# Grouped attention's weighted sums with the weights stationary and the values moving, on one Trainium2 core

## The chip, the core and the metric

The program runs on one core of a Trainium2 chip. The core has five engines that run their own instruction streams: TensorE (PE, matrix multiplications; the loading of its stationary operand is listed apart as PEld), VectorE (DVE), ScalarE (ACT), GpSimd (POOL) and SyncE (SP, which here only issues transfers). TensorE writes into PSUM, eight banks of 128 x 512 floats here; VectorE and ScalarE read PSUM and write SBUF. The metric is the device time of one execution in microseconds; several executions are timed and their median is taken. One execution is also recorded by the hardware profiler, and every row below comes from that record.

## The reference, cut to what matters

The model is a trunk of four layers with 256 positions and 2048 features. Layer 0 and layer 3 use latent attention; layer 1 uses grouped attention over keys that an indexer selects ("sparse"); layer 2 uses grouped attention in a sliding window with a learned sink per head. Each layer also has four heads of cross-attention to a memory, and the joined head outputs are multiplied by SiLU(gate) and projected back.

The change is in layers 1 and 2 alone. Both have 32 query heads of 64 features in 4 groups; the 8 heads of a group share one key head and one value head. For one head, in the window layer:

```python
s = q @ k.T * 64**-0.5 + bias          # 256 x 256, masked
m = max(rowmax(s), sink)
e = exp(s - m)
p = e / (rowsum(e) + exp(sink - m))    # a factor per row (query)
o = p @ v                              # weighted sum of the values, 256 x 64
...
y = concat(o of all heads, memory heads) * silu(gate)
x = x + y @ w_out
```

The factor of a row is the same for all keys of that row, so it can stand before or after the product with v. The sparse layer has no sink and takes its mask from the selection.

## The kernel before

Everything is computed in two parts of reduced width: a float32 matrix is split into a high part `hi` (what the type fp32r keeps) and a low part `lo` (the rest), by `split` (L58 to L64): ScalarE copies into `hi` (L60), VectorE subtracts (L64). A product is then hi*hi + hi*lo + lo*hi, three matrix multiplications in fp32r. The weights of every projection are split in that way on the fly: SyncE loads them (`stage`), `parts_of` makes `wh` and `wl` (three buffers each), and `rows_by` (L227 to L229) or `columns_by` (L246, L250) multiplies. These projections are most of TensorE's work.

For grouped attention the class `Grouped` has `first` (keys, values, and in the sparse layer the selection), `project(g)` (queries, the table of biases and the gate of group g) and `attend(g)`. A layer does memory part 4, groups 0 to 3, memory part 5, and after each part the output projection `w_out` of the part before it. No order of instructions is written out by hand here: the framework's planner sets the order on each engine before the program runs, from its own costs, earlier lines of the program first where their operands are ready. So the heads of a group are spread among the matrix multiplications of the previous part's `w_out` and of the next group's `project`.

`attend` handles one head at a time, the queries in two halves b of 128 (the second half has two key tiles, the first only one, because of causality):

- scores (L786, L789) in PSUM tiles `sp`;
- `masked_softmax` (L434): bias, row minimum of the negated scores (L445, L447), exponential with row sums (L452), reciprocal of the sums `rc` (L468 with a sink, L470 without), then `normalized`: ScalarE multiplies each half of `e` by its rows' factors (two ACTIVATE e<-e,rc through L60);
- `weights_T` (L427): three transposes of 128x128 blocks by TensorE into the PSUM tile `ptp`, float32;
- split of `ptp` into `pT` (high, ScalarE) and `hl` (low, VectorE), 128 x 384 each, keys on the partitions;
- the weighted sums (L811): six matrix multiplications into PSUM `o`. The values are stationary: `vz` is a buffer per part, with zero columns between the value heads so that a slice of 128 columns gives the head's 64 features either in the lower or in the upper half of the 128 output partitions (head pairs stack). The transposed weights move: 256 columns for key tile 0, 128 for key tile 1, each three times (hi*hi, hi*lo, lo*hi). The result has features on the partitions and queries along the columns, which is the layout of the gate;
- after four heads, `gated` (L415): `o` times the gate, and split into `y`.

PSUM has four buffers `mp` for `sp`, `ptp`, `o` and the transposes of the queries, and four `acc` for the projections. `o` is held over four heads. The tags of the work buffers that matter: `e` (4 buffers of 128 x 256: u, e, bs, th), `z` (3, used by the gate), `t512` (3).

`first` zeroes both `vz` with GpSimd (L689, 128 x 1152 elements each) and splits the values into them.

Of the kernel before, what the change touches and what calls it, by code (L numbers as in the profile page):

```python
# [8 lines left out]
F32 = mybir.dt.float32  # L9
F32R = mybir.dt.float32r  # L10
# [5 lines left out]
P = 128  # L16
S = 256
# [14 lines left out]
def kernel(ctx: ExitStack, tc: tile.TileContext, a: dict, out: bass.AP,  # L32
                             kinds=(0, 1, 2, 0)):
    nc = tc.nc
# [3 lines left out]
    act = ctx.enter_context(tc.tile_pool(name="act", bufs=1))  # L38
    wk = ctx.enter_context(tc.tile_pool(name="wk", bufs=1))
# [3 lines left out]
    def misc(name, dt=F32):  # L43
        return ps.tile([P, 512], dt, name=name, tag="mp", bufs=4)

    def tmp(name, n=512, dt=F32):
        return wk.tile([P, n], dt, name=name, tag=f"t{n}", bufs=3)

    def small(name, n, dt=F32, bufs=None):
        return wk.tile([P, n], dt, name=name, tag=f"s{n}" if bufs is None else name,  # L50
                       bufs=bufs or 6)

    def f32(ap):
        return ap.bitcast(F32)

    def part_tile(dt=F32R):
        return wk.tile([P, 512], dt, name="hl", tag="hl", bufs=3)

    def copy_act(o, i, scale=1.0):
        nc.scalar.activation(o, i, AF.Copy, scale=scale)  # L60

    def split(hi, lo, src):
        copy_act(hi, src)
        nc.vector.tensor_sub(lo, src, f32(hi))  # L64
# [19 lines left out]
    ident = cst.tile([P, P], F32, name="ident")  # L84
# [328 lines left out]
    def gated(y, o, gT, j):  # L413
        yt = tmp("yt")
        nc.vector.tensor_mul(yt, o, gT[:, j:j + 2, :].rearrange("p a b -> p (a b)"))  # L415
        y3 = yt.rearrange("p (a b) -> p a b", a=2)
        split(y[:, 0, j:j + 2, :], y[:, 1, j:j + 2, :], y3)


    def normalized(e, r, n):  # L420
        copy_act(e[:, :n], e[:, :n], scale=r)

    def weights_T(es, blocks):

        tp = misc("ptp")
        for i, (b, k) in enumerate(blocks):
            nc.tensor.transpose(tp[:, i * P:(i + 1) * P], es[b][:, k * P:(k + 1) * P], ident)  # L427
        return tp

    def attend(o, v, pT):  # L430
        nc.tensor.matmul(o, v[0], pT[:, :S], start=True, stop=False)
        nc.tensor.matmul(o[:, P:], v[1], pT[:, S:S + P], start=False, stop=True)

    def masked_softmax(score, bias, scale=None, nsk=None):  # L434


        es = []
        mn, sm = small("mn", 2), small("sm", 2)
        for b in range(2):
            n = (b + 1) * P  # L440
            sp = score(b)
            u = wk.tile([P, S], F32, name="u", tag="e", bufs=4)
            bi = bias(b, n)
            if b == 0:
                nc.vector.tensor_add(u[:, :n], sp[:, n:2 * n], bi)  # L445
                bi = u[:, :n]
            nc.vector.tensor_tensor_reduce(u[:, :n], sp[:, :n], bi, -1.0,  # L447
                                           nsk if nsk is not None else BIG,
                                           op0=OP.add, op1=OP.min, accum_out=mn[:, b:b + 1])
            e = wk.tile([P, S], F32, name="e", tag="e", bufs=4)  # L450
            if scale is None:
                nc.scalar.activation(e[:, :n], u[:, :n], AF.Exp, bias=mn[:, b:b + 1], scale=-1.0,  # L452
                                     accum_out=sm[:, b:b + 1])
            else:
                ms = small("ms", 2)
                nc.vector.tensor_mul(ms[:, :1], mn[:, b:b + 1], scale[0][:, b:b + 1])
                nc.scalar.activation(e[:, :n], u[:, :n], AF.Exp, bias=ms[:, :1],
                                     scale=scale[1][:, b:b + 1], accum_out=sm[:, b:b + 1])
            es.append(e)
        r = small("rc", 2)  # L460
        if nsk is not None:
            d = small("sd", 2)
            nc.vector.tensor_scalar(d, mn, nsk, None, op0=OP.subtract)
            e2 = small("se", 2)
            nc.scalar.activation(e2, d, AF.Exp)
            s3 = small("sa", 2)
            nc.vector.tensor_add(s3, sm, e2)
            nc.vector.reciprocal(r, s3)  # L468
        else:
            nc.vector.reciprocal(r, sm)  # L470
        for b in range(2):
            normalized(es[b], r[:, b:b + 1], (b + 1) * P)
        return weights_T(es, [(0, 0), (1, 0), (1, 1)])


# [188 lines left out]
    class Grouped:  # L664
# [7 lines left out]
        def first(self):  # L672
            nm, w = self.nm, self.w
            acc = rows_by(nm.at, 16, w, 0, (self.kv0, 512), "kv")
            self.k = act.tile([P, 4, 2, S], F32R, name="kd", tag="big0")
            vs = act.tile([P, 4, S], F32, name="vs", tag="aux", bufs=AUX)
            self.v, self.sel = vs[:, :2, :], vs[:, 2:, :]
            for t in range(2):
                sc = nm.col("rstd", t)
                self.dup(lambda i0, i1: self.k.rearrange("p g v s -> p (g v) s")  # L680
                         [:, i0:i1, t * P:(t + 1) * P], acc[t][:, :S], sc, 4)
                copy_act(self.v[:, t, :], acc[t][:, S:], scale=sc)
            if self.sparse:
                self.select()


            self.vz = [act.tile([P, 2, 9 * 64], F32R, name="vz", tag=f"big{1 + z}") for z in range(2)]
            for z in range(2):
                nc.gpsimd.memset(f32(self.vz[z]), 0.0)  # L689
            for t in range(2):  # L690
                hi, lo = (self.vz[z][:, t, 64:].rearrange("p (g c) -> p g c", c=P)[:, :, :64] for z in range(2))
                split(hi, lo, self.v[:, t, :].rearrange("p (g c) -> p g c", c=64))

        def dup(self, dst, src, sc, n):

# [83 lines left out]
        def attend(self, g, q, bm, gT):  # L779
            y = act.tile([P, 2, 4, S], F32R, name="y", tag="y", bufs=2)  # L780
            for h in range(8):
                def score(b):
                    sp = misc("sp")
                    qb = q[h // 4][:, h % 4, b * P:(b + 1) * P]
                    if b == 0:
                        nc.tensor.matmul(sp[:, :S], qb, self.k[:, g, :, :P], start=True, stop=True)  # L786
                    else:
                        for v in range(2):
                            nc.tensor.matmul(sp[:, :S], qb, self.k[:, g, v, :],  # L789
                                             start=v == 0, stop=v == 1)  # L790
                    return sp

                def bias(b, n):
                    bh = bm[:, h, S - n:]
                    if not self.sparse:
                        return bh
                    bs = wk.tile([P, S], F32, name="bs", tag="e", bufs=4)
                    nc.vector.tensor_add(bs[:, :n], bh, self.sel[:, b, :n])
                    return bs[:, :n]
                nsk = None if self.sparse else nsink[:, g * 8 + h:g * 8 + h + 1]  # L800
                tp = masked_softmax(score, bias, None, nsk)
                pH, pL = wk.tile([P, 512], F32R, name="pT", tag="pT", bufs=2), part_tile()
                split(pH[:, :3 * P], pL[:, :3 * P], tp[:, :3 * P])
                if h % 4 == 0:
                    o = misc("o")
                c0 = (h // 2 % 2) * S
                v0 = g * P + (64 if h % 2 == 0 else 0)
                for t in range(2):
                    ks = slice(t * S, t * S + S - t * P)
                    for n_, (z, p_) in enumerate(((0, pH), (0, pL), (1, pH))):  # L810
                        nc.tensor.matmul(o[:, c0 + t * P:c0 + S], self.vz[z][:, t, v0:v0 + P], p_[:, ks],  # L811
                                         start=h % 2 == t == n_ == 0, stop=h % 2 == t == 1 and n_ == 2)
                if h % 4 == 3:
                    gated(y, o, gT, (h // 4) * 2)
            return y


# [3 lines left out]
    for i in range(depth):  # L821
# [23 lines left out]
        for n_, part in enumerate(order):  # L845
            if part >= 4:
                y = memory_attend(*memory_project(nm, i, mixer.w, mixer.mq0, mixer.g0, part - 4))
            else:
                y = mixer.attend(*mixer.project(part))
# [89 lines left out]
```

## Time and profile before

| | |
|---|---|
| Median of 3 runs | 2635.05 us (2634.15 to 2639.67) |
| Profiled execution, its own time | 2636.8 us |
| Its span, first to last instruction | 2634.7 us |
| TensorE busy | 2601.2 us (99%) |
| VectorE busy | 1884.1 us (72%) |
| ScalarE busy | 1628.8 us (62%) |
| GpSimd busy | 57.3 us (2%) |
| Mean granted TensorE clock | 0.997 |
| Heads of grouped attention, sparse layer | about 1144 to 1484 us from the span's start |
| The same, window layer | about 1640 to 1976 us |

How to read it: a matrix multiplication's duration in a row is from its start to its modelled end, and several are in flight at once, so durations don't add up; what one costs TensorE is the step from its start to the start of the next. A row of the timeline with "x2" holds two consecutive instructions of the same line. "128x256" behind a multiplication is its output, so 256 moving columns. A load (LDWEIGHTS) runs beside the multiplication before it.

### The profile page before, as it was taken

How to read it: one execution, taken by the hardware profiler on the slowest of the kernel's cores; microseconds unless marked ns; L12 is line 12 of the kernel's file. 1: busy time of each engine (PE TensorE's matmuls, PEld its weight loads, DVE VectorE, ACT ScalarE, POOL GpSimd, SP SyncE). 2: the span in 40 equal slices, each digit the busy share in tenths (PEclk: the TensorE clock that was granted, in tenths of full speed). 3: DMA queues.
4: the chain of work that ended last, by engine and by line, in shares of the span. 5: the costliest groups of instructions: out<-in, count | busy, mean ns of one | idle time of the engine just before them, and what ended most of it. 6: DMA issues, size and time to landing. Idle time of an engine off the chain costs nothing.

```text
span 2634.7 us, 42943 instructions
## 1 busy us (share of the span) xinstructions
PE 2601.2 (99%) x14556; PEld 2254.7 (86%) x14556; DVE 1884.1 (72%) x4171; ACT 1628.8 (62%) x3476; POOL 57.3 (2%) x101
## 2 busy tenths in 40 slices
PE   8999999999999999999999999999999999999998
PEld 7888888888888889888888888888888888888886
DVE  6566656677767685877777776777778767776767
ACT  6455556556656566666666666676666655665655
POOL 1000000000000000000000000000000000000000
PEclk9999999999999999999999999999999999999999
DMA  9889886666557665555555555555555666655764
GB/s 305 279 287 300 281 256 198 166 185 168 169 160 224 192 192 172 167 183 170 173 163 191 188 190 177 173 172 178 189 168 162 205 165 186 165 170 156 226 183 135
DMA packets 456924, 511.70 MB, mean 194 GB/s; under 512 B 69584, under 2 KB 352480, under 8 KB 455552
## 3 DMA queue, kind: packets, MB, share of 16 engines
q1 hardware_dynamic: 443328, 451.75, 56.5%
q0 software_dynamic: 13088, 56.16, 6.6%
q8 instruction: 114, 1.87, 0.3%
q14 instruction: 106, 0.87, 0.1%
q10 hardware_dynamic: 288, 1.05, 0.1%
HBM read 489.91 MB, written 31.56 MB: 198 GB/s over the span
## 4 chain that ended last, share of the span: by engine, by line
PE 97%; DMA 1%; DVE 1%; ACT 0%; issue 0%; SPq 0%; ACTq 0%
PE acc_g L246 14%; PE acc_g L250 7%; PE acc_wo L227 7%; PE acc_wo L228 7%; PE acc_wo L229 7%; PE acc_mq L246 5%; PE acc_mk L246 5%; PE acc_qn L246 3%; PE acc_cq L246 3%; PE acc_mq L250 2%; PE acc_mk L250 2%; PE acc_q L227 2%; PE acc_q L228 2%; PE acc_q L229 2%; PE acc_mv L227 2%; PE acc_mv L228 2%
## 5 line engine op out<-in xcount | busy, mean ns | idle before, releaser
L64 DVE TENSOR_TENSOR wl<-wr,wh 128x512 fp32r<-128x512 f32 (+2 forms) x1776 | 1173.8, 664 | 645.1 <-ACT wh L60 614.2
L60 ACT ACTIVATE wh<-wr 128x512 fp32r<-128x512 f32 (+2 forms) x1776 | 1079.0, 609 | 837.3 <-PE acc_g L246 183.7
L246 PE MATMUL acc_g<-xT,wh 128*128 128x512 f32 x1536 | 489.0, 397 | 0.6 <-DVE z L257 0.6
L250 PEld LDWEIGHTS acc_g<-xT,wl 128*128 128x128 f32 x1536 | 285.2, 188 | 60.7
L250 PE MATMUL acc_g<-xT,wl 128*128 128x256 f32 x1536 | 311.0, 280 | 0.0
L228 PE MATMUL acc_wo<-wl,y 128*128 128x512 f32 x768 | 302.6, 394 | 0.6 <-DVE wl L64 0.5
L229 PE MATMUL acc_wo<-wh,y 128*128 128x512 f32 x768 | 299.1, 390 | 0.0
L246 PEld LDWEIGHTS acc_g<-xT,wh 128*128 128x128 f32 x1536 | 238.1, 189 | 4.8 <-issue 1.1
L227 PE MATMUL acc_wo<-wh,y 128*128 128x512 f32 x768 | 240.4, 393 | 0.7 <-ACT wh L60 0.6
L228 PEld LDWEIGHTS acc_wo<-wl,y 128*128 128x128 f32 x768 | 144.3, 188 | 30.0 <-DVE wl L64 1.4
L229 PEld LDWEIGHTS acc_wo<-wh,y 128*128 128x128 f32 x768 | 144.2, 188 | 28.4
L227 PEld LDWEIGHTS acc_wo<-wh,y 128*128 128x128 f32 x768 | 141.3, 188 | 27.8 <-ACT wh L60 1.0
L246 PE MATMUL acc_mk<-mT,wh 128*128 128x512 f32 x512 | 161.9, 398 | 2.4 <-ACT wh L60 2.4
L246 PE MATMUL acc_mq<-xT,wh 128*128 128x512 f32 x512 | 161.7, 397 | 0.0
L832 DVE TENSOR_TENSOR x<-x,acc_wo 128x512 f32<-128x512 f32 x192 | 125.7, 683 | 7.1 <-PE acc_wo L229 6.8
L246 PE MATMUL acc_qn<-cT,wh 128*128 128x512 f32 x384 | 123.2, 399 | 0.0
L246 PE MATMUL acc_cq<-xT,wh 128*128 128x512 f32 x384 | 120.8, 396 | 0.0
L250 PEld LDWEIGHTS acc_mk<-mT,wl 128*128 128x128 f32 x512 | 96.7, 189 | 23.4 <-DVE wl L64 0.8
L250 PEld LDWEIGHTS acc_mq<-xT,wl 128*128 128x128 f32 x512 | 93.7, 188 | 20.0
L250 PE MATMUL acc_mq<-xT,wl 128*128 128x256 f32 x512 | 102.5, 281 | 0.0
L228 PE MATMUL acc_q<-wl,xT 128*128 128x512 f32 x256 | 102.4, 400 | 0.0
L250 PE MATMUL acc_mk<-mT,wl 128*128 128x256 f32 x512 | 101.7, 280 | 0.0
(280 smaller groups left out, 4438.0 us busy)
## 6 DMA issues: line engine op xcount, KB each, us to landing
wr<-in_w_out_dram SPq DMA_DIRECT2D x192, 512.0 KB, 3.7
wr<-in_w_in_a_dram SPq DMA_DIRECT2D x176, 512.0 KB, 4.1
wr<-in_w_mem_kv_dram SPq DMA_DIRECT2D x128, 512.0 KB, 5.6
wr<-in_w_in_b_dram SPq DMA_DIRECT2D x112, 512.0 KB, 3.5
wr<-in_w_in_c_dram SPq DMA_DIRECT2D x104, 512.0 KB, 3.5
wr<-in_w_uq_dram SPq DMA_DIRECT2D x288, 128.0 KB, 2.6
tab<-flat POOLq DMA_DIRECT2D x8, 1536.0 KB, 11.1
wr<-in_w_in_a_dram SPq DMA_DIRECT2D x32, 288.0 KB, 3.0
```

The costliest lines, as they stand in the source:

```text
L60: nc.scalar.activation(o, i, AF.Copy, scale=scale)
L64: nc.vector.tensor_sub(lo, src, f32(hi))
L227: nc.tensor.matmul(acc[t][:, :n], xh, wh[:, :n], start=first, stop=False)
L228: nc.tensor.matmul(acc[t][:, :n], xh, wl[:, :n], start=False, stop=False)
L229: nc.tensor.matmul(acc[t][:, :n], xl, wh[:, :n], start=False, stop=last)
L246: nc.tensor.matmul(acc[j], wh[:, o:o + P], q[:, :, kt % 4, :], start=kt == 0, stop=False)
L250: nc.tensor.matmul(acc[j][:, 0, :], wl[:, o:o + P], q[:, 0, kt % 4, :], start=False, stop=kt == kts - 1)
L832: nc.vector.tensor_add(xs, xs, acc[t])
```

## The change

The weighted sums are turned round. The transposed weights `pH`, `pL` become the stationary operand, one 128 x 128 block per load, and the values' parts move: `vv` holds for each group 64 columns of the high part and 64 of the low part side by side, so one multiplication with `pH` stationary and 128 moving columns gives hi*hi and hi*lo in two halves, and one with `pL` stationary and 64 moving columns adds lo*hi to the second half. Three blocks per head give again six multiplications. The result now has queries on the partitions. So the rows' factor can be applied to the sums instead of to `e`: `normalized` is no longer called for these heads. After two heads ScalarE copies the second halves out of PSUM (`lo`), VectorE adds the first halves (`su`) and multiplies by the factors into `yr`; after four heads four transposes by TensorE (float32, into a PSUM tile `ot`) bring the layout with features on the partitions back, and `gated` reads `ot` instead of `o`. `o` is allocated every two heads. `vz` and its zeroing by GpSimd go.

```diff
-    def masked_softmax(score, bias, scale=None, nsk=None):
+    def masked_softmax(score, bias, scale=None, nsk=None, r=None):
...
-        r = small("rc", 2)
+        later = r is not None
+        if not later:
+            r = small("rc", 2)
...
-        for b in range(2):
-            normalized(es[b], r[:, b:b + 1], (b + 1) * P)
+        if not later:
+            for b in range(2):
+                normalized(es[b], r[:, b:b + 1], (b + 1) * P)
...
-            self.vz = [act.tile([P, 2, 9 * 64], F32R, name="vz", tag=f"big{1 + z}") for z in range(2)]
-            for z in range(2):
-                nc.gpsimd.memset(f32(self.vz[z]), 0.0)
-            for t in range(2):
-                hi, lo = (self.vz[z][:, t, 64:].rearrange("p (g c) -> p g c", c=P)[:, :, :64] for z in range(2))
-                split(hi, lo, self.v[:, t, :].rearrange("p (g c) -> p g c", c=64))
+            self.vv = act.tile([P, 2, 4, 2, 64], F32R, name="vv", tag="big1")
+            for t in range(2):
+                split(self.vv[:, t, :, 0, :], self.vv[:, t, :, 1, :],
+                      self.v[:, t, :].rearrange("p (g c) -> p g c", c=64))
...
             for h in range(8):
+                if h % 2 == 0:
+                    o = misc("o")[:].rearrange("p (b h v d) -> p b h v d", b=2, h=2, v=2)
+                    r = small("rc4", 4, bufs=3)[:].rearrange("p (b h) -> p b h", b=2)
+                if h % 4 == 0:
+                    yr = tmp("yr")[:].rearrange("p (b h d) -> p b h d", b=2, h=4)
...
-                tp = masked_softmax(score, bias, None, nsk)
+                tp = masked_softmax(score, bias, None, nsk, r[:, :, h % 2])
                 pH, pL = wk.tile([P, 512], F32R, name="pT", tag="pT", bufs=2), part_tile()
                 split(pH[:, :3 * P], pL[:, :3 * P], tp[:, :3 * P])
-                if h % 4 == 0:
-                    o = misc("o")
-                c0 = (h // 2 % 2) * S
-                v0 = g * P + (64 if h % 2 == 0 else 0)
-                for t in range(2):
-                    ks = slice(t * S, t * S + S - t * P)
-                    for n_, (z, p_) in enumerate(((0, pH), (0, pL), (1, pH))):
-                        nc.tensor.matmul(o[:, c0 + t * P:c0 + S], self.vz[z][:, t, v0:v0 + P], p_[:, ks],
-                                         start=h % 2 == t == n_ == 0, stop=h % 2 == t == 1 and n_ == 2)
+                for n_, (b, t) in enumerate(((0, 0), (1, 0), (1, 1))):
+                    ks = slice(n_ * P, (n_ + 1) * P)
+                    nc.tensor.matmul(o[:, b, h % 2].rearrange("p v d -> p (v d)"), pH[:, ks],
+                                     self.vv[:, t, g].rearrange("p v d -> p (v d)"),
+                                     start=t == 0, stop=False)
+                    nc.tensor.matmul(o[:, b, h % 2, 1, :], pL[:, ks], self.vv[:, t, g, 0, :],
+                                     start=False, stop=t == b)
+                if h % 2 == 1:
+                    lo = wk.tile([P, S], F32, name="ol", tag="z", bufs=3)[:].rearrange(
+                        "p (b h d) -> p b h d", b=2, h=2)
+                    su = wk.tile([P, S], F32, name="os", tag="z", bufs=3)[:].rearrange(
+                        "p (b h d) -> p b h d", b=2, h=2)
+                    copy_act(lo, o[:, :, :, 1, :])
+                    nc.vector.tensor_add(su, lo, o[:, :, :, 0, :])
+                    nc.vector.tensor_mul(yr[:, :, h % 4 - 1:h % 4 + 1, :], su,
+                                         r[:, :, :, None].to_broadcast([P, 2, 2, 64]))
                 if h % 4 == 3:
-                    gated(y, o, gT, (h // 4) * 2)
+                    ot = misc("ot")
+                    for j in range(2):
+                        for b in range(2):
+                            nc.tensor.transpose(ot[:, j * S + b * P:j * S + (b + 1) * P],
+                                                yr[:, b, 2 * j:2 * j + 2, :].rearrange("p h d -> p (h d)"),
+                                                ident)
+                    gated(y, ot, gT, (h // 4) * 2)
```

## Prediction

> **What bounds the kernel now.** I read the page's totals and its chain of waits first, then the busy times of the two stretches in which grouped attention runs, then who waited for whom there, and last the timeline of single instructions, because only steps from start to start price a matrix multiplication.
>
> ```profile
> span 2634.7 us, 42943 instructions
> ...
> PE 2601.2 (99%) x14556; PEld 2254.7 (86%) x14556; DVE 1884.1 (72%) x4171; ACT 1628.8 (62%) x3476; POOL 57.3 (2%) x101
> ...
> PE 97%; DMA 1%; DVE 1%; ACT 0%; issue 0%; SPq 0%; ACTq 0%
> ```
>
> ```profile
> core 0: us, PE busy (x) PEld busy (x) DVE busy (x) ACT busy (x) POOL busy (x), PEclk, DMA share, GB/s
> 1144.00:1554.00 410.00, 407.03 (x2210) 347.45 (x2209) 315.32 (x732) 268.26 (x592) 8.37 (x11) 1.00 0.56 177
> 1637.00:2036.00 399.00, 396.97 (x2207) 341.34 (x2206) 304.89 (x730) 266.54 (x623) 5.93 (x9) 1.00 0.55 173
> ```
>
> TensorE is busy 99% of the span and makes up 97% of the chain that ended last. In the two stretches with the heads it is idle for 410.00 - 407.03 + 399.00 - 396.97 = 5.0 us of 809, at full clock. VectorE is busy (315.32 + 304.89) / 809 = 77%, ScalarE 66%. So work that leaves or joins VectorE and ScalarE is worth nothing by itself; what counts is the time that TensorE needs for its instructions, and the few waits it has. Those of the stretch from 1144 to 2036 us, by engine and line, total, times and longest:
>
> ```profile
> PE o L811 <- ACT pT L60: 1.7, 3, 0.6
> PE ptp L427 <- ACT e L60: 1.4, 3, 0.5
> PE acc_g L246 <- DVE z L257: 0.6, 3, 0.2
> PE acc_wo L227 <- ACT wh L60: 0.6, 1, 0.6
> PE acc_wo L228 <- DVE wl L64: 0.5, 1, 0.5
> ```
>
> They are small: the planner has put projection work between the links of a head's chain nearly everywhere.
>
> **The weighted sums.** Moving columns per head go from 3 x 256 + 3 x 128 = 1152 to 3 x 128 + 3 x 64 = 576, loads stay at six. The timeline of one head's six multiplications and of their loads:
>
> ```profile
> 1195.86 0.39 PE L229 MATMUL acc_q<-wh,xT 128*128 128x512 f32 x1
> 1196.09 0.28 PE L811 MATMUL o<-pT,vz 128*128 128x256 f32 x1
> 1196.20 0.28 PE L811 MATMUL o<-hl,vz 128*128 128x256 f32 x1
> 1196.32 0.34 PE L811 MATMUL o<-pT,vz 128*128 128x256 f32 x2
> 1196.50 0.28 PE L811 MATMUL o<-hl,vz 128*128 128x128 f32 x1
> 1196.61 0.28 PE L811 MATMUL o<-pT,vz 128*128 128x128 f32 x1
> 1196.72 0.68 PE L227 MATMUL acc_q<-wh,xT 128*128 128x512 f32 x2
> 1197.24 0.40 PE L228 MATMUL acc_q<-wl,xT 128*128 128x512 f32 x1
> ```
>
> ```profile
> 1196.44 0.19 PEld L811 LDWEIGHTS o<-hl,vz 128*128 128x128 f32 x1
> 1196.55 0.19 PEld L811 LDWEIGHTS o<-pT,vz 128*128 128x128 f32 x1
> 1196.66 0.30 PEld L227 LDWEIGHTS acc_q<-wh,xT 128*128 128x128 f32 x2
> ```
>
> A multiplication with 512 columns takes 1196.09 - 1195.86 = 0.23 us from start to start. From the head's first multiplication to the acc_q of L228 at 1197.24, 1.15 us pass, of which the two acc_q of L227 would take 0.46 in a row: the six cost 0.69 us. With 256 columns the step is 0.115 us; with 128 columns it isn't half of that but 0.11 (1196.50 to 1196.61), because the loads follow each other no closer than 0.11 us. Halving the columns therefore buys almost nothing: six loads at 0.11 are 0.66 us. No row shows 64 moving columns in this type; the nearest on either side are the 128 columns above and a sum over features that moves a single column, four in a row:
>
> ```profile
> 478.55 0.53 PEld L592 LDWEIGHTS cqp<-ones,cqs 128*128 128x128 f32 x4
> 479.00 0.30 PEld L246 LDWEIGHTS acc_mq<-xT,wh 128*128 128x128 f32 x2
> ```
>
> (479.00 - 478.55) / 4 = 0.113 us per load with one column, so 0.11 to 0.113 holds from both ends, and six cost 0.66 to 0.68 us. I take 0.665, a gain of 0.025 us per head, 64 heads: 1.6 us (0.6 to 1.9).
>
> **The transposes of the sums.** Two layers x 32 heads / 4 x 4 = 64 float32 transposes of 128x128 more, the same operation as `ptp`. Four in a row by the timeline:
>
> ```profile
> 1991.84 0.60 PE L427 MATMUL ptp<-ident,e 128*128 128x128 f32 x4
> 1992.19 0.70 PE L227 MATMUL acc_wo<-wh,y 128*128 128x512 f32 x2
> 1992.73 0.39 PE L228 MATMUL acc_wo<-wl,y 128*128 128x512 f32 x1
> ```
>
> 1992.73 - 1991.84 - 2 x 0.23 = 0.43 us for four, x 16 = 6.9 us. They fill TensorE's own queue and nothing covers them. The row gives each a duration of 0.27 us behind the start of the last, but it overlaps what follows. [...]
>
> TensorE's sum: 6.9 - 1.6 = +5.3 us.
>
> **ScalarE, VectorE, GpSimd.** Rows of the groups kept apart by shape (busy us, mean ns of one):
>
> ```profile
> L60 ACT ACTIVATE e<-e,rc 128x256 f32<-128x256 f32 x128 | 61.9, 495 | 0.0
> L406 DVE TENSOR_TENSOR hz<-z,half 128x256 f32<-128x256 f32 x96 | 40.5, 422 | 1.5
> L257 DVE TENSOR_TENSOR z<-z,acc_g 128x256 f32<-128x256 f32 x96 | 39.8, 415 | 1.6 <-ACT z L60 1.6
> L60 ACT ACTIVATE e<-e,rc 128x128 f32<-128x128 f32 x96 | 37.4, 390 | 1.2 <-DVE rc L468 0.9
> L60 ACT ACTIVATE z<-acc_g 128x256 f32<-128x256 f32 x96 | 35.2, 367 | 0.0
> L689 POOL MEMSET vz<- 128x1152 f32 x4 | 4.2, 1063 | 158.1 <-PE isp L745 130.9 <-ACT rl L748 16.9 <-PE o L811 10.3
> ```
>
> Gone per pair of heads: four e<-e,rc, 2 x (0.495 + 0.390) = 1.77 us of ScalarE. New: `lo`, like z<-acc_g, 0.37 on ScalarE; `su`, like z<-z,acc_g, 0.42, and the product with the factors, like hz<-z,half, 0.42 on VectorE (the strided and the broadcast operand have no row of exactly this form; between 0.42 and twice that). Over 32 pairs ScalarE loses 45 us and VectorE gains 27 (to 54), which makes it (620 + 27) / 809 = 80%, 83% at the upper bound. TensorE covers both. The cover is thinnest where heads and `w_out` fall together:
>
> ```profile
> 1164.00:1184.00 20.00, 20.00 (x97) 16.70 (x97) 17.02 (x41) 12.58 (x28) 0.00 (x0) 1.00 0.58 184
> ```
>
> There VectorE already has 17.0 of 20 us; one pair more of products is 17.9, still under 20, with three buffers of `wl` ahead of TensorE. I book nothing. The four memsets (1.06 us) and their waits are GpSimd's alone, whose queue otherwise only issues transfers; nobody in the list of TensorE's waits waits for it. The split of the values has as many elements as before. Nothing on SP's queue moves.
>
> **Waits.** The transposes of `e` no longer wait for ScalarE's product with `rc`: the row of 1.4 us goes, and the head's chain is 0.9 us shorter. Against it, TensorE's queue now holds 16 times four transposes that wait for `lo`, `su`, the product: three links of 0.37 + 0.42 + 0.42 = 1.2 us and what stands ahead of them in two queues (0.6 to 0.7 us per split of the weights), and behind them in TensorE's queue stand the projection and the next head's scores. If the planner puts them too near, TensorE stands still. What such a misplacement costs, in the rows where `o` waited for `pT`:
>
> ```profile
> 1303.79 0.38 PE L427 MATMUL ptp<-ident,e 128*128 128x128 f32 x2
> 1304.75 0.38 PE L811 MATMUL o<-pT,vz 128*128 128x256 f32 x1 [0.58 <-ACT pT L60]
> 1305.33 0.47 PE L246 MATMUL acc_g<-xT,wh 128*128 128x512 f32 x1 [0.20 <-DVE z L257]
> ```
>
> 0.58 us, at 3 of 64 heads. With three links instead of one I take 3 of 16 places at 0.6 us: 1.9 us; bounds are none (0) and all 16 (9.6 us). Sum of waits: +1.9 - 1.4 = +0.5 us, from -5.0 (all idle time of the stretches goes) to +9.6.
>
> **Sum.** 5.3 + 0.5 = +5.8 us. The profiled execution's own time is 2636.8 us, 1.8 above the median; +5.8 makes 2642.6 for an execution like it, and 2635.05 + 5.8 = 2640.9 for the median. About 0.2% (5.3 us) is what a measurement of this kernel can tell from no change, so the forecast lies just beyond that edge.
>
> **Rivals.**
> - *The new waits bite.* TensorE waits at most of the 16 places, or the extra VectorE work makes `wl` late in the stretch of 17 of 20 us. For it: VectorE's load there and the three-link chain. Against it: TensorE's waits in this trace are few. Price: 16 x 0.6 instead of 1.9 gives +7.7 more, 2648.6; I give the case 2643.5 to 2655.
> - *The shorter chain pays.* A head without the two products ends earlier, and the waits at the groups' ends go. At best 5.0 us of idle time: 2635.05 + 5.3 - 5.0 = 2635.4, no change.
> - *Faster: columns pace the multiplications, not loads.* If the loads of the turned operands hide fully, a head's 576 columns cost 576 x 0.23 / 512 = 0.26 us instead of 0.69: 64 x 0.43 = 27.5 us less, 6.9 more, 2614.4. It breaks even where the six cost 0.69 - 6.9 / 64 = 0.58 us, and is faster by 0.2% at 0.50. Against it stand the steps of 0.11 us at 128 columns and at one. [...]
> - *The transposes cost their full duration*, 64 x 0.27 = 17.3 instead of 6.9 us: 2651.3. The four in 0.43 us speak against it.
>
> **How the numbers follow.** Forecast (2638.5 to 2643.5) 0.45, of which 0.28 lies above 2640.3 and 0.17 below. New waits 0.26, full transposes 0.05: slower. Shorter chain 0.16: same. Columns pace 0.08: faster. So slower 0.28 + 0.26 + 0.05 = 0.59, same 0.33, faster 0.08. The range 2634 to 2652 leaves out the columns' case (0.08) and the far end of the waits and transposes (some 0.07). The likeliest case's own range is 2638.5 to 2643.5.
>
> **What would show it.** In the changed kernel's timeline: loads of the six at steps of 0.11 us and 0.66 us per head; four transposes of `yr` in 0.43 us; ScalarE's busy time 45 us lower, VectorE's 27 higher; no wait of `ptp` for e<-e,rc; a new row in which `ot` waits for VectorE, of about 2 us in total. The prediction is wrong if six cost under 0.6 us, if `ot` or acc_wo waits sum to more than 5 us, or if the planner lays the heads out so differently that idle time appears where none is now.

## The result, and the profile after

The changed kernel takes 2661.88 us (median of 5, 2658.87 to 2665.77), the one before 2635.05: a ratio of 1.0102, with a 95% interval from 1.0091 to 1.0114. It is slower by 27 us. The forecast was 2640.9, its range ended at 2652, so the direction was right and the size was not.

The totals and the chain of waits of the profiled execution (its own time is 2658.87 us):

```profile
span 2657.0 us, 43016 instructions
...
PE 2616.2 (98%) x14620; PEld 2266.5 (85%) x14620; DVE 1906.5 (72%) x4235; ACT 1593.4 (60%) x3380; POOL 53.1 (2%) x97
...
PE 96%; DMA 2%; DVE 1%; ACT 1%; issue 0%; SPq 0%; ACTq 0%
```

TensorE is busy 15 us more and idle about 7 us more (2657.0 - 2616.2 = 40.8 against 33.5). VectorE has 22 us more, ScalarE 35 us less (27 and 45 were forecast). Where the rest went shows in no total but in slices of 5 us. These are two stretches at the ends of the layers, while the last heads of the last group run; the columns are those of the stretches view in the prediction, and the first number behind the five busy times is the granted clock:

```profile
1445.00:1450.00 5.00, 5.00 (x35) 4.50 (x34) 4.76 (x13) 2.74 (x6) 0.00 (x0) 1.00 0.44 114
1450.00:1455.00 5.00, 3.82 (x25) 3.11 (x23) 3.68 (x12) 3.37 (x10) 0.00 (x0) 1.00 0.64 200
1455.00:1460.00 5.00, 3.23 (x18) 2.72 (x18) 2.99 (x11) 2.25 (x8) 1.44 (x2) 0.83 0.13 27
1460.00:1465.00 5.00, 3.29 (x12) 2.14 (x10) 2.36 (x7) 0.88 (x2) 0.00 (x0) 0.50 0.82 292
1465.00:1470.00 5.00, 5.00 (x22) 4.43 (x22) 2.89 (x7) 0.63 (x1) 0.00 (x0) 0.65 0.00 0
```

```profile
1955.00:1960.00 5.00, 3.66 (x24) 2.76 (x22) 3.53 (x14) 3.72 (x14) 0.00 (x0) 1.00 0.51 163
1960.00:1965.00 5.00, 3.88 (x17) 3.35 (x17) 2.77 (x12) 2.02 (x7) 0.54 (x1) 0.50 0.28 79
1965.00:1970.00 5.00, 3.87 (x13) 2.92 (x14) 3.21 (x10) 0.39 (x1) 0.00 (x0) 0.50 0.07 25
1970.00:1975.00 5.00, 5.00 (x22) 4.42 (x22) 2.01 (x5) 0.76 (x2) 0.00 (x0) 0.63 0.01 3
```

TensorE goes idle for 22 to 35% of the time, ScalarE and VectorE thin out too, and then the granted clock falls to 0.50 and stays there after the work has come back (1465 to 1470: TensorE busy all the time at 0.65). From the clock column the half speed lasted 5 x (0.17 + 0.50 + 0.35) / 0.5 = 10.2 us at the first end and 5 x (0.50 + 0.50 + 0.37) / 0.5 = 13.7 us at the second. The kernel before has a clock of 1.00 in all slices of either place. In slices of 0.5 us the clock column reads 0.77 from 1458.0 and 0.53 from 1960.0 us, with 1.00 before and 0.50 behind, so it falls at 1458.27 and at 1960.03. In the 5 us ahead of each fall TensorE was busy for 2.91 and 3.63 us (58 and 73%). What sets the fall and its length these rows don't show.

Why TensorE had no work shows in VectorE's and ScalarE's timeline in the first of the two stretches. `head_parts` takes the queries of memory part 5 out of PSUM: ScalarE copies the high part (mqT), VectorE makes the rest through a buffer `zl`.

```profile
1438.72 0.64 ACT L60 ACTIVATE mqT<-acc_mq 128x256 fp32r<-128x256 f32 x2
...
1452.35 0.64 ACT L60 ACTIVATE mqT<-acc_mq 128x256 fp32r<-128x256 f32 x2
...
1462.78 0.39 ACT L60 ACTIVATE ol<-o 128x256 f32<-128x256 f32 x1 [1.96 <-PE o L817]
```

```profile
1463.20 0.42 DVE L825 TENSOR_TENSOR os<-ol,o 128x256 f32<-128x256 f32 x1 [1.79 <-ACT ol L60]
1463.54 0.42 DVE L265 TENSOR_TENSOR zl<-acc_mq,mqT 128x256 f32<-128x256 f32 x1
1463.87 0.41 DVE L826 TENSOR_TENSOR yr<-os,rc 128x256 f32<-128x256 f32 x1
1464.20 0.42 DVE L265 TENSOR_TENSOR zl<-acc_mq,mqT 128x256 f32<-128x256 f32 x1
```

ScalarE's first two copies stand at 1438.72, all are done by 1453; VectorE, idle for 1.79 us just before, makes the first `zl` only at 1463.54, 25 us behind the first copies and right behind the `su` (named `os` in the profile) of the very last pair of heads. `zl`, `ol` and `os` share the tag `z`. Until `zl` is made, the four `acc` banks of PSUM stay full, the gate's projection can't start (its first acc_g stands at 1465.00, right behind the first mqT<-zl,acc_mq at 1464.54), and there is nothing to put between the links of the last heads.

TensorE's waits from 1144 to 2060 us:

```profile
PE o L814 <- ACT pT L60: 5.6, 9, 0.8
PE tr L395 <- DVE hl L715: 2.4, 6, 0.4
PE ot L832 <- DVE yr L826: 2.0, 2, 1.0
PE ptp L427 <- ACT e L453: 2.0, 4, 1.0
PE o L817 <- DVE hl L64: 1.3, 6, 0.3
```

### The profile page after: what moved, and what is told of

It reads as the page before. It is cut to its first block, busy times and chain, and to the rows that moved or that the text cites. A ratio compares the mean times of both kernels' runs of the same rounds, so it can differ in the third digit from the quotient of the medians.

```text
span 2657.0 us, 43016 instructions
## 1 busy us (share of the span) xinstructions
PE 2616.2 (98%) x14620; PEld 2266.5 (85%) x14620; DVE 1906.5 (72%) x4235; ACT 1593.4 (60%) x3380; POOL 53.1 (2%) x97
## 4 chain that ended last, share of the span: by engine, by line
PE 96%; DMA 2%; DVE 1%; ACT 1%; issue 0%; SPq 0%; ACTq 0%
PE acc_g L246 14%; PE acc_g L250 7%; PE acc_wo L228 7%; PE acc_wo L227 7%; PE acc_wo L229 7%; PE acc_mq L246 5%; PE acc_mk L246 4%; PE acc_qn L246 3%; PE acc_cq L246 3%; PE acc_mq L250 2%; PE acc_q L228 2%; PE acc_q L227 2%; PE acc_q L229 2%; PE acc_mk L250 2%; PE acc_mv L227 2%; PE acc_mv L228 2%
```

## The experiments

Theory A, formed from these rows: the planner hands out the buffers of a tag in the order of the program's lines. `lo` and `su` of all heads of a group stand ahead of the next part's drains in the program, so a drain gets no `z` buffer until the last pair of heads has had its two. Theory B: the heads' longer chain on VectorE and ScalarE is late by itself.

**Own buffers for `lo` and `su`.**

```diff
-                    lo = wk.tile([P, S], F32, name="ol", tag="z", bufs=3)[:].rearrange(
+                    lo = wk.tile([P, S], F32, name="ol", tag="sco0", bufs=1)[:].rearrange(
...
-                    su = wk.tile([P, S], F32, name="os", tag="z", bufs=3)[:].rearrange(
+                    su = wk.tile([P, S], F32, name="os", tag="sco1", bufs=1)[:].rearrange(
```

> The changed kernel with `lo` and `su` in two buffers of their own (those of the selection's scores, idle here) instead of the three of the tag `z`, which the drains of the gate and of the memory queries use too. Theory A (buffers of a tag are handed out in the program's order, so `zl` of the memory queries, later in the program than `lo` and `su` of the last heads, gets none until the last pair is summed, and TensorE runs out of projection work): `zl` follows mqT<-acc_mq within 2 us instead of 25, the granted clock stays at 1.00 near 1460 and 1965 us, and the time falls from 2662 to 2638 to 2645 us. Theory B (the heads' longer chain on VectorE and ScalarE is late by itself, whatever buffers it uses): no change, 2656 to 2666 us.

Measured: 2638.33 us, ratio to before 1.0012 (1.0002 to 1.0021). `zl` now comes with the copies, and TensorE is full. VectorE's timeline and the slices at the same place:

```profile
1454.88 0.74 DVE L265 TENSOR_TENSOR zl<-acc_mq,mqT 128x256 f32<-128x256 f32 x2
```

```profile
1455.00:1460.00 5.00, 5.00 (x33) 4.38 (x33) 4.81 (x15) 3.42 (x9) 0.00 (x0) 1.00 0.60 195
1460.00:1465.00 5.00, 5.00 (x33) 4.43 (x33) 3.48 (x6) 2.80 (x6) 0.00 (x0) 1.00 0.42 123
```

23.6 of the 26.8 us are gone with a change of two tags. Theory A holds for the changed kernel. Theory B doesn't hold as it is put (late whatever buffers the heads use); that the chain's length matters too is shown further down.

**The same buffers taken in the kernel before.** Added ahead of `gated`:

```diff
+                if h % 2 == 1:
+                    lo = wk.tile([P, S], F32, name="ol", tag="z", bufs=3)
+                    su = wk.tile([P, S], F32, name="os", tag="z", bufs=3)
+                    copy_act(lo[:, :1], o[:, c0:c0 + 1])
+                    nc.vector.tensor_add(su[:, :1], lo[:, :1], o[:, c0:c0 + 1])
```

> The kernel before, with one thing added: after every second head one column of `o` is copied by ScalarE into a `z` buffer and added by VectorE into a second one (results unused). That takes `z` buffers in the order of the changed kernel with 0.2 us of work per pair and none of its turned products. Theory A: the drains wait as in the changed kernel, clock dips appear near the ends of both layers, 2648 to 2658 us. Theory B: 2634 to 2639 us, as before.

Measured: 2699.73 us, ratio 1.0244 (1.0229 to 1.0260). Two one-column instructions per pair of heads cost 64 us, where 13 to 23 were expected. The same two instructions in tags of their own weren't run, so what they cost besides the buffers isn't split off. The starved stretch appears behind the earlier groups too (first row below), not only at the layer's end:

```profile
1225.00:1235.00 10.00, 7.56 (x41) 6.33 (x41) 6.49 (x18) 6.53 (x19) 0.91 (x1) 0.83 0.38 126
...
1470.00:1475.00 5.00, 3.91 (x15) 2.63 (x13) 3.04 (x13) 2.59 (x9) 0.08 (x1) 0.50 0.00 0
1475.00:1480.00 5.00, 3.75 (x14) 3.02 (x14) 1.50 (x5) 2.50 (x8) 1.36 (x2) 0.50 0.58 177
1480.00:1485.00 5.00, 2.62 (x9) 2.08 (x9) 3.38 (x10) 0.80 (x2) 2.05 (x2) 0.50 0.39 143
```

**Number of buffers, or order?** All of `z`, with the selection's two buffers (and the sum of squares `cqs` that used one of them) moved into it:

```diff
-tag="z", bufs=3
+tag="z", bufs=5
...
-name=f"sco{z}", tag=f"sco{z}", bufs=1
+name=f"sco{z}", tag="z", bufs=5
```

> The changed kernel with five buffers in the tag `z` instead of three (the selection's two moved into it), `lo` and `su` still in `z`: as many buffers in all as in the kernel with own ones. It tells the number of buffers from the order in which they are handed out. If it is the order (a later line of the program gets none before the earlier ones have theirs): `zl` still waits for the last pair, the clock still dips, 2653 to 2666 us. If it is the number: 2636 to 2643 us.

Measured: 2666.14 us, ratio 1.0114 (1.0098 to 1.0129). As many buffers in all as in the first experiment, and nothing gained. The starved stretches stand at the same two places, some 5 us later:

```profile
1465.00:1470.00 5.00, 3.27 (x11) 2.51 (x12) 3.22 (x11) 0.39 (x1) 0.00 (x0) 0.50 0.54 192
...
1970.00:1975.00 5.00, 3.29 (x11) 2.54 (x12) 3.24 (x10) 0.39 (x1) 0.00 (x0) 0.50 0.00 0
```

From 1080 to 1130 us, where the selection runs, TensorE stays busy (49.7 of 50 us), so the time wasn't lost to the selection's buffers instead. It is the order.

**Which drain.** `zl` of the grouped layers' memory queries in the selection's two buffers, the rest of the changed kernel as it is:

```diff
-    def head_parts(dst, acc):
+    def head_parts(dst, acc, own=False):
...
-            z = wk.tile([P, S], F32, name="zl", tag="z", bufs=3)
+            if own:
+                z = wk.tile([P, S], F32, name="zl", tag=f"sco{j}", bufs=1)
+            else:
+                z = wk.tile([P, S], F32, name="zl", tag="z", bufs=3)
...
-            head_parts(q, acc)
+            head_parts(q, acc, kinds[i] != 0)
```

> The changed kernel, `lo` and `su` left in `z`, but the memory queries' `zl` in the two grouped layers in two buffers of its own. Only the drain at the ends of the layers is freed, the gates' drains are not. If the two ends (17 us of the difference by the traces) hang on `zl` alone: 2640 to 2646 us, clock at 1.00 near 1460 and 1965 us. If another drain stands behind it, the gate's `z` for one: the dips move later or stay, 2650 us or more.

Measured: 2668.04 us, ratio 1.0121 (1.0106 to 1.0136). This lies outside both ranges. The slices at the layers' ends are full at a clock of 1.00, but a new hole has opened where the selection runs:

```profile
1080.00:1090.00 10.00, 3.53 (x17) 3.19 (x17) 8.85 (x34) 3.74 (x11) 0.00 (x0) 0.72 0.14 48
1090.00:1100.00 10.00, 3.17 (x13) 2.18 (x12) 8.64 (x23) 2.69 (x7) 0.00 (x0) 0.67 0.00 1
1100.00:1110.00 10.00, 4.41 (x13) 3.76 (x14) 6.88 (x22) 0.00 (x0) 0.00 (x0) 0.50 0.01 2
...
1476.00:1486.00 10.00, 10.00 (x65) 8.84 (x63) 8.80 (x25) 6.66 (x16) 0.00 (x0) 1.00 0.49 148
```

The reading is that in memory part 4 `zl` now stood behind the selection's scores for their buffers: the same collision in another tag. With the own buffers in part 5 alone (the edit is against the run before it):

```diff
-            head_parts(q, acc, kinds[i] != 0)
+            head_parts(q, acc, kinds[i] != 0 and part == 1)
```

> The changed kernel with `zl` in buffers of its own only in memory part 5, the one behind the last group, so that part 4 doesn't meet the selection's buffers. `lo` and `su` and the gates' drains still share `z`. If the two ends hang on `zl`: 2640 to 2647 us, no clock dip near 1460 and 1965 us; what then remains over the kernel with own buffers for `lo` and `su` (2638) is the gates' part, 0 to 6 us. If the ends have another cause: 2655 us or more.

Measured: 2642.85 us, ratio 1.0031 (1.0021 to 1.0041). Both the hole at the selection and the two at the ends are gone; at the first end, for example:

```profile
1460.00:1465.00 5.00, 5.00 (x33) 4.43 (x32) 3.48 (x6) 2.80 (x6) 0.00 (x0) 1.00 0.48 138
```

So 19.0 us (2661.9 - 2642.9) hang on `zl` at the two ends. For the 4.5 us left to the own buffers (2638.3) the cause isn't shown. No row of this trace has TensorE waiting for the gate's `z`. It has the row of `tr` (the transposes of the queries) waiting for `hl`, 2.4 us at six places, as the changed kernel has; the list with own buffers has none.

**VectorE's load by itself.** Own buffers, `su` and the product with the factors each done twice.

```diff
                     nc.vector.tensor_add(su, lo, o[:, :, :, 0, :])
+                    nc.vector.tensor_add(su, lo, o[:, :, :, 0, :])
+                    nc.vector.tensor_mul(yr[:, :, h % 4 - 1:h % 4 + 1, :], su,
+                                         r[:, :, :, None].to_broadcast([P, 2, 2, 64]))
```

> The first kernel of this set (own buffers) with VectorE's sum `su` and its product with the factors each done twice, 27 us more of VectorE work in the two layers. Theory A: within 3 us of the single one, since TensorE covers it. Theory B: 8 us or more slower than the single one.

Measured: 2638.60 us, ratio 1.0011 (1.0001 to 1.0021), 0.3 us from the single one, with VectorE busy 21 us longer in the two stretches (657.1 against 636.0). That VectorE has room was right.

**The transposes.** Own buffers, `gated` reads `yr`; the heads' sums go into the gate in the wrong layout.

```diff
-                    ot = misc("ot")
...
-                    gated(y, ot, gT, (h // 4) * 2)
+                    gated(y, yr.rearrange("p b h d -> p (b h d)"), gT, (h // 4) * 2)
```

> The first kernel of this set (own buffers) without the 64 transposes of the sums: `gated` reads `yr` itself, so the heads' sums go into the gate in the wrong layout. This prices the transposes and the wait for them. By the prediction's row (0.43 us for four) 6.9 us less than with them, and 1 to 3 us more if the wait at `ot` counts: 2632 to 2637 us under theory A. At 0.27 us each it would be 17 us less.

Measured: 2629.37 us, ratio 0.9977 (0.9967 to 0.9986), 9.0 us less than with the transposes by the medians, each known to some 2.6 us. TensorE's busy time fell by 7.2 us (2606.3 to 2599.1), near the 6.9 of the row. The list of waits with own buffers has no row for `ot`, so a wait for the transposes isn't shown.

**The chain without the factors.** The kernel before, grouped layers without `normalized`:

```diff
-        for b in range(2):
-            normalized(es[b], r[:, b:b + 1], (b + 1) * P)
+        if scale is not None:
+            for b in range(2):
+                normalized(es[b], r[:, b:b + 1], (b + 1) * P)
```

> The kernel before without the two products with the rows' factors in the grouped layers (the sums are left unnormalized there). It prices the shorter chain by itself, with TensorE's work unchanged: 45 us less of ScalarE. If ScalarE and the chain are covered: 2632 to 2637 us; if the chain's length sets TensorE's waits, up to 5 us less than before, 2630 us.

Measured: 2626.25 us, ratio 0.9968 (0.9958 to 0.9978): 9 us less by the medians (the interval of the ratio gives 6 to 11), more than any case named. In its trace TensorE has no wait left from 1144 to 2036 us; the list is empty, and TensorE is busy in the whole of both stretches. That is the 5.0 us of idle time, and the two traced executions are 5.2 us apart (2634.7 against 2629.5); no trace shows where more than that comes from.

**The factors back in the changed kernel** (own buffers, the products with `rc` kept, so the factors count twice):

```diff
-        if not later:
-            for b in range(2):
-                normalized(es[b], r[:, b:b + 1], (b + 1) * P)
+        for b in range(2):
+            normalized(es[b], r[:, b:b + 1], (b + 1) * P)
```

> The changed kernel with own buffers for `lo` and `su` (2638 us), and the two products e<-e,rc by ScalarE put back into each head (the factors are then applied twice, so the sums are wrong). It prices the shorter chain inside the changed kernel. If it is worth there what it is in the kernel before (8.4 us): 2645 to 2649 us. If nothing, because other waits take its place: 2638 to 2641 us.

Measured: 2666.73 us, ratio 1.0118 (1.0103 to 1.0134). In the changed kernel the shorter chain is worth 28 us, not 8. TensorE's waits of this run from 1144 to 2060 us:

```profile
PE o L813 <- ACT pT L60: 5.8, 9, 0.8
PE acc_wo L227 <- DVE z L257: 3.7, 6, 2.9
PE acc_g L246 <- DVE z L257: 2.7, 5, 0.9
PE acc_wo L227 <- ACT wh L60: 2.6, 7, 0.5
...
```

All waits of that list sum to 20 us, against 3.7 with own buffers and the short chain. Two of the rows are projections that wait for the gate's drain (z L257): banks held too long again, though this time no buffer of `z` is taken by the heads. The trace has a candidate. The gate's `th` shares the tag `e` with `u`, `e` and `bs` of the heads. At the end of the window layer `th` starts 17.8 us behind the `hz` that it reads (1975.12 to 1992.92), right behind the last head's exponential (1992.42). With own buffers and the short chain the same gap is 0.5 us, in the kernel before it is 10.4 us (1956.95 to 1967.31) and there without the factors 0.5 us. That looks like the same collision in a third tag; no run gave `th` a tag of its own, so it isn't shown.

**The one-column use with the short chain.** The second experiment without `normalized` in the grouped layers.

> The kernel before with the one-column use of two `z` buffers per pair (2700 us) and without the two products with the rows' factors in the grouped layers (the sums are left unnormalized). It asks why the one-column use cost 64 us in the kernel before and the same buffers 19 to 24 us in the changed one. If it is the heads' length (with the products, the last pair of a group ends later, so the drains behind it wait longer in every group): about the changed kernel less its transposes, 2648 to 2662 us, and no clock dips in groups 0 to 2. If the length doesn't matter: 2690 us or more.

Measured: 2640.04 us, ratio 1.0017 (1.0007 to 1.0026), 60 us below the same with the products, and below the range expected. The clock dips are where they were expected: at the two ends, none behind the earlier groups. What the one-column use of `z` costs is 14 us with the short heads (2640.0 against 2626.3) and 64 with the long ones, so the heads' length decides what the order of buffers costs. That a pair which ends late frees its drain late is the reading of it.

**Two heads wide.** What the trace says on loads, used in the kernel before: heads that share a slice of `vz` move together.

```diff
-            for h in range(8):
+            for n8, h in enumerate((0, 2, 1, 3, 4, 6, 5, 7)):
...
+                if n8 % 2 == 0:
+                    pH = wk.tile([P, 2, 3 * P], F32R, name="pT2", tag="pT", bufs=2)
+                    pL = wk.tile([P, 2, 3 * P], F32R, name="hl2", tag="hl", bufs=3)
+                split(pH[:, n8 % 2, :], pL[:, n8 % 2, :], tp[:, :3 * P])
...
+                if n8 % 2 == 1:
+                    v0 = g * P + (64 if h % 2 == 0 else 0)
+                    o3 = o[:].rearrange("p (h s) -> p h s", h=2)
+                    for t in range(2):
+                        ks = slice(t * S, t * S + S - t * P)
+                        for n_, (z, p_) in enumerate(((0, pH), (0, pL), (1, pH))):
+                            nc.tensor.matmul(o3[:, :, t * P:], self.vz[z][:, t, v0:v0 + P], p_[:, :, ks],
...
```

(To make room, the selection's scores and the sum of squares of layers 0 and 3 move into the tag `t512`, the rotary parts `qrs` into `hl`.)

> The kernel before with the heads of a group taken two at a time, 0 and 2, 1 and 3 and so on, which share the same slice of `vz`: one multiplication moves both heads' columns, 512 and 256 instead of 256 and 128, so two heads take six multiplications and loads instead of twelve. If loads pace the narrow ones (0.11 us at 128 columns, as many as at 1) and columns the wide ones, two heads cost 3 x 0.23 + 3 x 0.115 = 1.03 us instead of 1.38: 32 x 0.35 = 11 us less than before, 2624 us, as long as heads that come in twos make no new waits (up to 2635 us if they do). If columns paced all of them, there would be no gain: 2635 us.

Measured: 2627.81 us, ratio 0.9974 (0.9963 to 0.9984). It is the fastest here that computes the whole result, faster than both kernels. Five of its six in a row on TensorE (the first pT, with 512 columns, stands earlier; the row with x2 holds one of 512 and one of 256):

```profile
1181.90 0.40 PE L814 MATMUL o<-hl,vz 128*128 128x512 f32 x1
1182.13 0.51 PE L814 MATMUL o<-pT,vz 128*128 128x512 f32 x2
1182.48 0.28 PE L814 MATMUL o<-hl,vz 128*128 128x256 f32 x1
1182.60 0.28 PE L814 MATMUL o<-pT,vz 128*128 128x256 f32 x1
1182.72 0.61 PE L227 MATMUL acc_q<-wh,xT 128*128 128x512 f32 x2
1183.17 0.39 PE L228 MATMUL acc_q<-wl,xT 128*128 128x512 f32 x1
```

1183.17 - 1181.90 - 0.46 = 0.81 us for five, 1.04 with the sixth at 0.23, as worked out. TensorE is busy 11.8 us less (2589.4 against 2601.2), the 11 us forecast; the medians are some 8 us apart. Projections now wait for the gate's drain (acc_g for z L257, 5.4 us at six places, where the kernel before has 0.6). What the buffers that moved to other tags are worth by themselves wasn't run.

**The factors inside the transposes**, on top of that:

```diff
+            dg = tmp("dgr")[:, :S].rearrange("p (b q) -> p b q", b=2)
+            nc.vector.tensor_scalar(dg[:, 0, :], ident, r[:, 0:1], None, op0=OP.mult)
+            copy_act(dg[:, 1, :], ident, scale=r[:, 1:2])
+            tp = misc("ptp")
+            for i, (b, k) in enumerate([(0, 0), (1, 0), (1, 1)]):
+                nc.tensor.matmul(tp[:, i * P:(i + 1) * P], es[b][:, k * P:(k + 1) * P], dg[:, b, :],
+                                 start=True, stop=True)
```

> Two heads at a time as in the wide kernel (2628 us), and the rows' factors taken out of the chain in another way than in the change: the three transposes of `e` become multiplications by a diagonal matrix of the factors, which VectorE makes for the first half (0.29 us) and ScalarE for the second (0.39 us) beside it, in place of 0.88 us of ScalarE in a row. TensorE's work stays (a float32 multiplication with 128 columns steps 0.11 us like the transpose). If the shorter chain pays as in the kernel without factors (8 us): 2621 to 2625 us. If the wide kernel has no waits left that it could save: 2626 to 2629 us; if the float32 multiplications cost more than the transposes, 2630 us or more.

Measured: 2645.07 us, ratio 1.0033 (1.0020 to 1.0046), 17 us slower than without. The instructions on `ptp` say why (count, then shortest, median and longest duration in ns):

```profile
L477 PEld LDWEIGHTS ptp<-dgr,e x384: 186/191/193, 1170.6 to 1975.2; 128*128 128x128 f32 x192
L477 PE MATMUL ptp<-dgr,e x384: 270/275/344, 1170.8 to 1975.3; 128*128 128x128 f32 x192
L427 PEld LDWEIGHTS ptp<-ident,e x160: 137/139/143, 524.6 to 2602.8; 128*128 128x128 f32 x160
```

192 products (64 heads, three each) are 384 multiplications with 384 loads: a float32 multiplication is two instructions here, a transpose is one (the wide kernel has 352 on `ptp`: the 192 that the products replace, and the 160 of the last row). The expectation had the step of one instruction right (six in a row take 1178.21 - 1177.31 - 0.23 = 0.67 us) and their number wrong. 192 more at 0.11 us are 21 us, and TensorE is busy 19.8 us longer than in the wide kernel (2609.2 against 2589.4). What the shorter chain gives here can't be read apart from that.

## Why the prediction was wrong, point by point

*Bound by TensorE, ScalarE and VectorE covered.* Right as to their work: doubling VectorE's new products changed the time by 0.3 us. ScalarE's busy time fell by 35 us (45 forecast), VectorE's rose by 22 (27 forecast). `su` and the product measured 0.42 and 0.41 us as taken, but an instruction starts 0.34 us behind the one before it (1463.20 to 1463.54 above), so that busy time counts less than the sum of the durations.

*Six multiplications, 0.665 us.* Right. In the changed kernel, five in a row:

```profile
1172.81 0.19 PE L817 MATMUL o<-vv,hl 128*128 128x64 f32 x1
1172.84 0.30 PE L814 MATMUL o<-vv,pT 128*128 128x128 f32 x1
1172.98 0.24 PE L817 MATMUL o<-vv,hl 128*128 128x64 f32 x1
1173.06 0.31 PE L814 MATMUL o<-vv,pT 128*128 128x128 f32 x1
1173.21 0.24 PE L817 MATMUL o<-vv,hl 128*128 128x64 f32 x1
1173.29 0.48 PE L228 MATMUL acc_wo<-wl,y 128*128 128x512 f32 x1
1173.60 0.39 PE L229 MATMUL acc_wo<-wh,y 128*128 128x512 f32 x1
```

1173.60 - 1172.81 - 0.23 = 0.56 us for five, 0.112 each, though half of them move 64 columns. The rival in which columns set the pace is out.

*Transposes, 6.9 us.* The instruction's price was right: 9.0 us by the medians, 7.2 of TensorE's busy time; the rival with 17.3 us is out. `ot` waited for `yr` 2.0 us in the changed kernel, where 1.9 was forecast. That is luck: it is two waits of 1.0 us instead of three of 0.6, both in the starved stretches at the two ends (1464.34 and 1968.46), and none is left with own buffers.

*Waits: 1.4 us gone with the products.* Mis-sized: the shorter chain is worth 9 us in the kernel before and 28 in the changed one with own buffers. The term took only the row of `ptp` waiting for e<-e,rc. In the kernel before, the waits of `o` for `pT` and of the projections for the gate's drain went with the products too. In the changed kernel the row of `ptp` came back as a wait for the exponential, 2.0 us.

*"I book nothing" for VectorE and ScalarE.* This is the step that failed. The new instructions were priced by their durations and by the engines' room, not by the buffers in which they write. `lo` and `su` take two of three `z` buffers, and the drains of PSUM behind them in the program wait until the last pair has had its own. The description of the kernel lists the tag and its three buffers; the argument never asked who waits for a buffer that the new instructions hold. No rival named it: the nearest, "the new waits bite", put the waits at `ot` and ended at 2655. The prediction's last sign of being wrong, idle time where none is now, is what came, though it was put down to the planner's layout and got no price. With own buffers the changed kernel takes 2638.3 us, 2.6 below the forecast of 2640.9; the shared buffers are the 23.6 us on top. No row of the list of waits before names a wait for a buffer of `z`, but that `zl` has the tag `z` could be read in the code, and in the timeline before, `th` of the tag `e` already stood 10.4 us behind its `hz`.

One path through the runs splits the difference: 2635.4 before; -9.1 us for the shorter chain; +3.1 for turned sums, `lo`, `su` and the product (to 2629.4); +9.0 for the transposes (2638.3); +23.6 for the shared buffers (2661.9). Each term is a difference of two medians that are known to some 2.6 us, so the +3.1 (-1.6 was forecast) can't be told from nothing. The terms add up because they are taken one behind the other; in another order they differ, since the shorter chain is worth 28 us where the sums are turned. The second and third term also hold whatever the planner's new order brings, which wasn't measured apart. How the 19 us at the two ends divide between TensorE idle and half clock wasn't measured either: by the slices TensorE is idle 4.7 us in 1450 to 1470 and 3.6 in 1955 to 1970, which leaves some 11 us to the clock, an estimate from these rows. It is near what the steps give: two acc_g, of 512 and 256 columns, take 0.64 us at a clock of 0.50 (1465.60 to 1466.24) and 0.35 us at 1.00 (1469.50 to 1469.85), and 0.29 / 0.64 of the 8.3 and 11.4 us that TensorE was busy at half clock is 8.9 us.

## What to carry to other kernels

When a change adds a temporary, ask whose buffers it takes: where a planner hands a tag's buffers out in the program's order, a late user in one part stops the PSUM drains of the next. Here neither two more shared buffers nor room on the engine helped; a tag of its own did, as long as no other user of that tag stood ahead, and a chain that ends sooner made the wait cheaper. On an engine that is busy 99% of the time, count its instructions with their loads, not the columns: multiplications of 64 and 128 columns with a new stationary block each took 0.11 us alike, and what gained was moving two heads under one load (TensorE busy 11.8 us less). And the holes of a few microseconds in TensorE's work cost about twice their length here (8.3 us of idle time in 19 us at the two ends): the granted clock fell to 0.50 at both.

## What the runs showed that was not expected

The granted clock fell to 0.50 behind 5 us in which TensorE had still been busy 58 and 73% of the time, and came back only 10 to 14 us later. Two one-column instructions per pair of heads cost 64 us (2699.7 against 2635.4). A float32 multiplication of 128x128 by 128x128 was two instructions with two loads (384 for 192 products), a float32 transpose of the same size one. Taking ScalarE's two products out of each head's chain saved 9 us by the medians (6 to 11) of a kernel whose TensorE was busy 99%; its rows showed 5.0 us of idle time in the two stretches.
